# Where adaLN's rows, the norms and an expert's pieces are bound in the order of a transformer layer's kernel

## The chip, the cores and the metric

The kernel runs on one core of a Trainium2 chip. The metric is the device time of one execution in microseconds (us). A core has five engines with a queue of instructions each, worked off in order: TensorE (PE, with its weight loads as PEld), VectorE (DVE), ScalarE (ACT), GpSimd (POOL) and SyncE (SP), which here issues most of the DMA transfers. An instruction that waits holds up all that stands behind it on its own engine, and nothing else directly.

## What is computed

One layer over 2048 latent tokens of width 1024, float32, with 256 context tokens. The reference, cut to its path:

```python
mod = silu(c) @ w_ada + b_ada
sh1, sc1, g1, sh2, sc2, g2 = split(mod, 6)
h = layernorm(x) * (1 + sc1) + sh1
q, k, v, u, vg, ga, gb = split(h @ w_in)
y_attn = windowed_attention(q, k, v, context keys and values, sink, mask)
vc = layernorm(gelu(vg), gm_ln_g, gm_ln_b)        # chunks of 128 tokens, 8 groups of 64
y_gm = gelu(u) * (einsum('gpq,nqgc->npgc', gm_ws, vc) + gm_bs)
mix = (sigmoid(ga) * (y_attn @ w_pa) + sigmoid(gb) * (y_gm @ w_pb)) @ w_o
x = layernorm(ALPHA * x + g1 * mix, ln1_g, ln1_b)
h2 = layernorm(x) * (1 + sc2) + sh2
x = layernorm(ALPHA * x + g2 * mixture_of_experts(h2), ln2_g, ln2_b)   # top 2 of 32
```

## The kernel before

**Stages.** A first pass (0 to about 600 us) normalises the tokens, projects q, k and v and does the attention; it leaves `hT_d` (the modulated tokens, transposed), `oT_d` (attention output) and `vg_d` in DRAM. The second pass, `pass2`, takes the 2048 tokens as four groups g = 0..3 of 512 tokens, four tiles of 128 each, and starts its group 0 at about 600 us, group 1 at about 785. Then come the experts: `early_block` for the first of them, and from about 1490 us the experts' loop.

**Products.** A float32 product is made of three products of rounded halves: `split` (line 85) casts a piece to its high half on ScalarE (`Wh`, `hh`, `gh`) and subtracts that on VectorE for the low half (`Wl`, `hl`, `gl`); `mm3` (lines 741 to 743) multiplies high by high, low by high and high by low. A matmul of line 742 therefore needs a `Wl`, one of 741 a `Wh`. Weights pass through `piece` (line 729): one buffer `raw` of 128 x 1024, of which there are three (`RAW`), loaded by a DMA that SP issues. `Wh` and `Wl` have three buffers each, the PSUM banks `mm` four, `tr` two.

**A group.** `head(g)` forms the projection u from four `raw` pieces of `hT_d` and four of `wu`; `gelu_u` and four `norm_v` (a load `vg`, GELU, statistics, `vg` normalised by lines 784 and 785, split into `yl`) feed `spatial`, which for each of eight groups of channels does a product into `tr` and then line 840 on VectorE, the product with u into `yh`. Then a loop over f = 0..7, one eighth of the merged width each: `gate(g, f + 1, 0)`, for f = 0 also `mixers(g)` (transposes of `yh` by line 850 and their split into `gh` and `gl`) and `attended(g)`, then `between(g, f)`, `gate(g, f + 1, 1)`, `merge` and `behind`. `out_proj` evacuates `mm` into `rr` (line 906) at the end of groups 0 to 2; the last group has a planner of its own, `last_tiles`.

**The two kinds of side work.** In group 0 `between` issues one step of `rows_ada`, for f = 0..5. A step forms 512 entries of g1, sh2 or sc2: four pieces of `w_ada` through the same `raw` ring, eight VectorE instructions into `aacc` (lines 760 and 762), a split into `ah` and `al`; two matmuls and an addition (lines 774 to 777) follow as `finish` when `between` is called next. In groups 1 to 3 `between` issues for f = 0..3 the `norms` of one tile of the group before: load `x`, line 912 (`rr<-x,rr`), a layer norm of `rr` (statistics of line 94, the small ones of 98 and 99, the root of line 100 on GpSimd, lines 784 and 785), a store, a second norm into `x` and a second store. From f = 1 on the transposes and logits of the tile before it follow.

**What sets the order.** The program is written out as above, and a scheduler then orders each engine's instructions by a simulated timeline. `tc.issue_after(ins)` adds one rule to it: instructions that are traced inside the block and run on the engine of `ins` may not be issued ahead of `ins`. `st["mixed"]` is the last split of `attended`, on VectorE. The norms of each tile are bound by

```python
with tc.issue_after(st["mixed"]):
    h2s[t] = norms(t, rr[f])
```

and the scheduler places that split early, ahead of the spatial products, so all the norms may go there as well.

**The experts' loop.** The blocks of up to 128 tokens follow one another expert by expert. `prepare(s, p)` loads the weight piece p of expert s (`mraw`, 1 MB) and splits it into `mWh` and `mWl`; `rows` makes the stationary operand `xh` of the next block, `hidden` and `output` are its matmuls (`terms`, line 1612). `k.at[kp]` is the last matmul of the kp-th quarter of `hidden`. In block 1 the loop calls `prepare(1, 0)` and `prepare(1, 1)`, with no rule on their order.

Of the kernel before, what the change touches and what calls it, by code (L numbers as in the profile page):

```python
# [13 lines left out]
OP = mybir.AluOpType  # L14
# [690 lines left out]
def pass2(k):  # L705
    nc, tc, T = k.nc, k.tc, k.T
    k.late = k.ctx.enter_context(tc.tile_pool(name="late", bufs=1, reuse_waits="tile"))
    with ExitStack() as ctx:
# [16 lines left out]
        bst = c.tile([P, 8], F32, name="bst")  # L725
# [25 lines left out]
        def rows_ada(dst, cb, one):  # L751

            acc = wk.tile([P, 512], F32, name="aacc", tag="aacc", bufs=1)
            for kp in range(4):
                w = piece(T["ada2"][cb, :, 2 * kp:2 * kp + 2, :].rearrange("p a b -> p (a b)"))
                for j in range(2):
                    kc = 2 * kp + j
                    ws = w[:, j * 512:(j + 1) * 512]
                    if kc == 0:
                        nc.vector.tensor_scalar(acc, ws, k.sil[:, kc, 0:1], None, op0=OP.mult)  # L760
                    else:
                        nc.vector.scalar_tensor_tensor(acc, ws, k.sil[:, kc, 0:1], acc, op0=OP.mult, op1=OP.add)
            ah = wk.tile([P, 512], F32R, name="ah", tag="th", bufs=1)
            al = wk.tile([P, 512], F32R, name="al", tag="tl", bufs=1)
            split(k, ah, al, acc)
            if dst is None:
                d = wk.tile([P, 512], F32, name="sg", tag="sg", bufs=2 * AHEAD + 2)
                nc.sync.dma_start(d, bcast_row(T["b_ada"][2048 + cb * 512:2048 + (cb + 1) * 512], 512))
            else:
                d = dst[:, (cb % 2) * 512:(cb % 2 + 1) * 512]  # L770

            def finish():
                pr = tr_bank()
                nc.tensor.matmul(pr, ones, ah, start=True, stop=False)
                nc.tensor.matmul(pr, ones, al, start=False, stop=True)
                nc.vector.scalar_tensor_tensor(d, d, one, pr, op0=OP.add, op1=OP.add)
                if dst is None:
                    nc.sync.dma_start(k.g2_d[:, (cb % 2) * 512:(cb % 2 + 1) * 512], d[0:1, :])
            return finish
# [7 lines left out]
        st = {}  # L787
# [41 lines left out]
        def spatial(g):  # L829

            uy, vv = st[g][1], st["vv"]
            if g == 0:
                tc.keep_in_program_order(nc.sync.dma_start(bst, T["bst"]))
            ws = wsplit(T["wst"].rearrange("p g q -> p (g q)"))
            for gg in range(8):
                tp = tr_bank()
                sp = tp[:, 0:256].rearrange("p (i d) -> p i d", d=HD)
                cs = slice(gg * HD, (gg + 1) * HD)
                mm3(sp, [x[:, gg * P:(gg + 1) * P] for x in ws], (vv[:, 0, :, cs], vv[:, 1, :, cs]), True, True)
                nc.vector.scalar_tensor_tensor(uy[:, 1, :, cs], sp, bst[:, gg:gg + 1], uy[:, 0, :, cs],  # L840
                                               op0=OP.add, op1=OP.mult)

        def mixers(g):

# [313 lines left out]
        rr, h2s, turned, routes, wout, due = None, {}, {}, {}, {}, []  # L1158

        def between(g, f):  # L1160

            nonlocal g1, sh2, sc2, ln1g, ln1b, rws
            while due:
                due.pop(0)()
            if g == 0:
                if f < 6:
                    due.append(rows_ada(g1 if f < 2 else sh2 if f < 4 else sc2, f, 1.0 if f // 2 == 2 else 0.0))
                return
            t = 4 * (g - 1) + f
            if 1 <= f < 5:  # L1170
                turned[t - 1] = logit_rows(h2s[t - 1])
            if f < 4:
                with tc.issue_after(st["mixed"]):
                    h2s[t] = norms(t, rr[f])
            if g == 1 and f in (5, 6):
                due.append(rows_ada(None, f + 1, 0.0))
# [310 lines left out]
def moe(k):  # L1487
    nc, tc, T = k.nc, k.tc, k.T
    with ExitStack() as ctx:
# [40 lines left out]
        def prepare(s, p):  # L1530

            if s >= NE:
                return
            hi, lo = (weight(n, s, p) for n in "hl")
            split(k, hi, lo, raws[s, p])
            parts[s, p] = (hi, lo)
            if s or p < 4:
                load()
# [164 lines left out]
        for i in range(NBL):  # L1703
            s, _, _, last = blocks[i]
            hidden(i)
            gate(i)
            with tc.issue_after(k.at[3]) if not i else nullcontext():
                rows(i + 1)
                if not i:
                    early_output(1)  # L1710
            if i:
                gather(i + GA)
                output(i - 1)
                evacuate(i - 1)
            if last:
                ahead(s, 3)
            if i and blocks[i - 1][3]:
                prepare(s, 4)
                prepare(s, 5)
            if i == 1:  # L1720
                prepare(1, 0)
                prepare(1, 1)
            if i > 3:
                next(k.tables, None)
        k.gb = wr.tile([P, 2, D], F32, name="gb", tag="mraw", bufs=RAWS)
# [184 lines left out]
```

## Time and profile before

| | us |
|---|---|
| median of three runs | 2355.22 |
| lowest and highest | 2352.29, 2355.99 |
| the profiled execution's own time | 2353.14 |
| span of the profile (first to last instruction) | 2351.1 |

The mean granted TensorE clock of that execution was 0.977 of full speed. PE was busy for 2206.8 us, DVE for 1749.7, ACT for 1197.9, POOL for 622.1. "Idle before" of a group of instructions is the time its engine stood idle ahead of them, and a wait is put down to the work that released it. Idle time of an engine that nobody waits for costs nothing, so the tables of TensorE's waits come first, and the other engines' order of time is read where they point to.

### The profile page before, as it was taken

The page shows a single profiled execution, that of the slowest core. Times are in us where ns is not written, and L with a number is a line of the kernel's source. Part 1 is how long each engine was busy: PE and PEld are TensorE (multiplying, and loading weights), DVE is VectorE, ACT ScalarE, POOL GpSimd, SP SyncE. Part 2 cuts the span into 40 slices and gives each one's busy share as a digit, 9 for nine tenths or more (in the row PEclk, how much of TensorE's full clock was granted, in tenths as well). Part 3 has the DMA queues.
Part 4 walks back from the last instruction along what each step waited for, and adds up shares of the span by engine and source line. Part 5 has one row for each costly group of instructions (what it writes and reads, how often), then busy time and mean ns, then how long its engine had stood idle before and what let it go on. Part 6 is the DMA issues. An engine that isn't in the chain of part 4 may idle for free. (4 is left out here: it accounts for less than half of the span.)

```text
span 2351.1 us, 31795 instructions
## 1 busy us (share of the span) xinstructions
PE 2206.8 (94%) x11269; PEld 1813.8 (77%) x11269; DVE 1749.7 (74%) x3029; ACT 1197.9 (51%) x1673; POOL 622.1 (26%) x518
## 2 busy tenths in 40 slices
PE   7899999999999999999999999899999999999980
PEld 3789999997778788878887887587877777877760
DVE  4778888887675677577557858578898878696977
ACT  3566666655433333333424333356666666564755
POOL 1333333331000101011101113323353445243324
PEclk9899999999999999999999999899999999999995
DMA  8111111115674446544344434489998989797967
GB/s 313 64 59 59 55 59 42 41 42 170 197 239 153 152 144 185 161 151 150 112 156 153 153 117 188 152 271 322 338 339 290 330 280 331 234 360 235 337 215 295
DMA packets 126710, 449.34 MB, mean 191 GB/s; under 512 B 20763, under 2 KB 42195, under 8 KB 101973
## 3 DMA queue, kind: packets, MB, share of 16 engines
q1 hardware_dynamic: 113684, 405.29, 49.8%
q0 software_dynamic: 12864, 41.98, 7.5%
q8 instruction: 90, 1.47, 0.3%
q14 instruction: 72, 0.58, 0.1%
HBM read 382.66 MB, written 64.57 MB: 190 GB/s over the span
## 5 line engine op out<-in xcount | busy, mean ns | idle before, releaser
L85 DVE TENSOR_TENSOR mWl<-mraw,mWh 128x2048 fp32r<-128x2048 f32 x192 | 450.2, 2362 | 89.9 <-ACT mWh L85 89.0
L85 ACT CAST mWh<-mraw 128x2048 fp32r<-128x2048 f32 x192 | 363.7, 1909 | 176.0 <-PE h L1612 82.2
L100 POOL TENSOR_TENSOR mv<-mv,mhalf 128x1 f32<-128x1 f32 x58 | 56.7, 981 | 664.2 <-DVE mv L99 657.9
L1612 PE MATMUL h<-mWh,xh 128*128 128x512 f32 x784 | 218.2, 400 | 12.4 <-ACT xh L85 7.9
L85 DVE TENSOR_TENSOR Wl<-raw,Wh 128x1024 fp32r<-128x1024 f32 x140 | 170.4, 1220 | 77.5 <-ACT Wh L85 76.8
L85 ACT CAST Wh<-raw 128x1024 fp32r<-128x1024 f32 x140 | 146.1, 1047 | 139.0 <-PE mm L743 66.2
L1612 PE MATMUL h<-mWl,xh 128*128 128x512 f32 x784 | 214.7, 394 | 0.0
L742 PE MATMUL mm<-hh,Wl 128*128 128x512 f32 x512 | 201.1, 393 | 5.5 <-DVE Wl L85 5.5
L741 PE MATMUL mm<-hh,Wh 128*128 128x512 f32 x512 | 202.7, 396 | 2.3 <-ACT Wh L85 1.6
L743 PE MATMUL mm<-hl,Wh 128*128 128x512 f32 x512 | 200.8, 392 | 0.0
L1660 POOL DMA_INDIRECT acc_d<-yo,lst x48 | 144.1, 3003 | 153.6 <-DVE yo L1654 95.7
L1612 PEld LDWEIGHTS h<-mWh,xh 128*128 128x128 f32 x784 | 145.3, 189 | 46.5 <-ACT xh L85 9.8
L1612 PEld LDWEIGHTS h<-mWl,xh 128*128 128x128 f32 x784 | 146.8, 188 | 32.9
L383 PE MATMUL pj<-wq,hTh 128*128 128x256 f32 (+1 forms) x544 | 151.9, 355 | 1.6 <-DVE hTh L364 1.4
L1577 POOL DMA_INDIRECT xg<-h_d,lst x48 | 79.9, 1665 | 206.6 <-PE tr L1598 98.7
L85 ACT CAST ph<-pt 128x512 fp32r<-128x512 f32 x184 | 93.4, 520 | 73.4 <-PE pt L572 69.9
L1612 PE MATMUL h<-mWh,xl 128*128 128x512 f32 x464 | 127.0, 394 | 0.0
L548 ACT ACTIVATE Sb<-Sb,mx 128x641 f32<-128x641 f32 (+1 forms) x128 | 105.4, 824 | 40.3 <-DVE mx L543 31.3
L541 DVE CUSTOM_DVE_ANT_0 Sb<-S,mask,sink 128x640 f32<-128x640 f32 (+1 forms) x128 | 110.2, 861 | 18.9 <-PE S L537 15.8
L85 DVE TENSOR_TENSOR pl<-pt,ph 128x512 fp32r<-128x512 f32 x184 | 109.0, 604 | 19.2 <-ACT ph L85 17.4
L1612 PE MATMUL y<-mWh,gh 128*128 128x512 f32 x392 | 112.2, 406 | 8.1 <-ACT mWh L85 3.3
L742 PEld LDWEIGHTS mm<-hh,Wl 128*128 128x128 f32 x512 | 96.7, 189 | 26.4 <-DVE Wl L85 7.1
(385 smaller groups left out, 5371.9 us busy)
## 6 DMA issues: line engine op xcount, KB each, us to landing
mraw<-mw SPq DMA_DIRECT2D x192, 1024.0 KB, 7.3
raw<-wf SPq DMA_DIRECT2D x96, 512.0 KB, 3.7
raw<-ada SPq DMA_DIRECT2D x32, 512.0 KB, 4.8
raw<-wo SPq DMA_DIRECT2D x32, 512.0 KB, 4.2
x<-x SPq DMA_DIRECT2D x30, 512.0 KB, 4.3
x<-ada SPq DMA_DIRECT2D x16, 512.0 KB, 5.4
hT_d<-hf SPq DMA_DIRECT2D x32, 256.0 KB, 2.2
raw<-hT_d SPq DMA_DIRECT2D x16, 512.0 KB, 4.9
```

The costliest lines, as they stand in the source:

```text
L85: return k.nc.scalar.copy(hi, src), (eng or k.nc.vector).tensor_sub(lo, src, hi)
L100: nc.gpsimd.tensor_tensor(mv[:, 3:4], mv[:, 2:3], k.mhalf, op=OP.pow)
L383: ins = nc.tensor.matmul(box[0][:, :n], x[:, kc, ts], wpart(y, kc, slice(c0, c0 + n))[:, 0, :], start=q == 0, stop=q == 3 * KC - 1)
L541: nc.vector.tensor_tensor_reduce(x[:, :nk], S[:, :nk], mask[:, mi, :nk], 1.0, sink[:, h:h + 1], OP.add, OP.max, mx[:, s:s + 1])
L548: nc.scalar.activation(Sb[s][:, :nk + 1], Sb[s][:, :nk + 1], AF.Exp, bias=mx[:, 2 + s:3 + s], scale=1.0, accum_out=mx[:, 4 + s:5 + s])
L741: nc.tensor.matmul(out, lh, rh, start=first, stop=False)
L742: nc.tensor.matmul(out, ll, rh, start=False, stop=False)
L743: nc.tensor.matmul(out, lh, rl, start=False, stop=last)
L1577: ins = nc.gpsimd.indirect_dma_start(out=xg[i][0:n, :], out_offset=None, in_=k.h2_d[:, :], in_offset=bass.IndirectOffsetOnAxis(ap=place(i) ...
L1612: ins = nc.tensor.matmul(accs[m], a[:, ks], b[:, c0:c0 + 512], start=first and i + j == 0, stop=last and j == 1 and i == len(t) - 1)
L1660: nc.gpsimd.indirect_dma_start(out=k.acc_d[:, :], out_offset=bass.IndirectOffsetOnAxis(ap=l[:, 0:1], axis=0), in_=yo[0:n, :], in_offset=No ...
```

## The change

There are three parts. In group 0 the six steps of `rows_ada` are issued at f = 1..6 in place of f = 0..5, and bound behind `st["sp"]`, which is new: the last VectorE instruction of line 840, the end of the group's spatial mixing. In groups 1 to 3 the norms for f = 1, 2 and 3 are bound behind `st["sp"]` too; the first tile's (f = 0) stay behind `st["mixed"]`. In the experts' loop `prepare(1, 0)` and `prepare(1, 1)` are bound behind `k.at[3]`, which in block 1 is the last matmul of that block's `hidden`.

```diff
--- before.py
+++ after.py
@@ -837,8 +837,8 @@
                 sp = tp[:, 0:256].rearrange("p (i d) -> p i d", d=HD)
                 cs = slice(gg * HD, (gg + 1) * HD)
                 mm3(sp, [x[:, gg * P:(gg + 1) * P] for x in ws], (vv[:, 0, :, cs], vv[:, 1, :, cs]), True, True)
-                nc.vector.scalar_tensor_tensor(uy[:, 1, :, cs], sp, bst[:, gg:gg + 1], uy[:, 0, :, cs],
-                                               op0=OP.add, op1=OP.mult)
+                st["sp"] = nc.vector.scalar_tensor_tensor(uy[:, 1, :, cs], sp, bst[:, gg:gg + 1], uy[:, 0, :, cs],
+                                                          op0=OP.add, op1=OP.mult).ins
 
         def mixers(g):
 
@@ -1163,14 +1163,15 @@
             while due:
                 due.pop(0)()
             if g == 0:
-                if f < 6:
-                    due.append(rows_ada(g1 if f < 2 else sh2 if f < 4 else sc2, f, 1.0 if f // 2 == 2 else 0.0))
+                if 1 <= f < 7:
+                    with tc.issue_after(st["sp"]):
+                        due.append(rows_ada(g1 if f < 3 else sh2 if f < 5 else sc2, f - 1, 1.0 if f > 4 else 0.0))
                 return
             t = 4 * (g - 1) + f
             if 1 <= f < 5:
                 turned[t - 1] = logit_rows(h2s[t - 1])
             if f < 4:
-                with tc.issue_after(st["mixed"]):
+                with tc.issue_after(st["sp" if f else "mixed"]):
                     h2s[t] = norms(t, rr[f])
             if g == 1 and f in (5, 6):
                 due.append(rows_ada(None, f + 1, 0.0))
@@ -1718,8 +1719,9 @@
                 prepare(s, 4)
                 prepare(s, 5)
             if i == 1:
-                prepare(1, 0)
-                prepare(1, 1)
+                with tc.issue_after(k.at[3]):
+                    prepare(1, 0)
+                    prepare(1, 1)
             if i > 3:
                 next(k.tables, None)
         k.gb = wr.tile([P, 2, D], F32, name="gb", tag="mraw", bufs=RAWS)
```

VectorE, group 0, around the last two spatial products (the rows of line 840), before. The `aacc` rows are the second step of `rows_ada` (f = 1), `Wl` a weight piece's low half, `gl` the first splits of `mixers`:

```order
L762 SCALAR_TENSOR_TENSOR aacc_7528<-raw_7533,sil_96,aacc_7528 128x512 x2
L762 SCALAR_TENSOR_TENSOR aacc_7528<-raw_7537,sil_96,aacc_7528 128x512
L85 TENSOR_TENSOR Wl_7494<-raw_7491,Wh_7493 128x1024
L762 SCALAR_TENSOR_TENSOR aacc_7528<-raw_7537,sil_96,aacc_7528 128x512
L887 TENSOR_TENSOR sg_7211<-sg_7211,mm_7458 128x512
L840 SCALAR_TENSOR_TENSOR yh_6994<-tr_7309,bst_6993,yh_6994 128x4x64
L840 SCALAR_TENSOR_TENSOR yh_6994<-tr_7314,bst_6993,yh_6994 128x4x64
L762 SCALAR_TENSOR_TENSOR aacc_7528<-raw_7541,sil_96,aacc_7528 128x512 x2
L85 TENSOR_TENSOR gl_7358<-tr_7352,gh_7357 128x512
L85 TENSOR_TENSOR Wl_7552<-raw_7549,Wh_7551 128x1024
L85 TENSOR_TENSOR gl_7358<-tr_7361,gh_7357 128x512
```

The same place after the change:

```order
L85 TENSOR_TENSOR Wl_7434<-raw_7431,Wh_7433 128x1024
L840 SCALAR_TENSOR_TENSOR yh_6994<-tr_7299,bst_6993,yh_6994 128x4x64
L840 SCALAR_TENSOR_TENSOR yh_6994<-tr_7304,bst_6993,yh_6994 128x4x64
L85 TENSOR_TENSOR Wl_7473<-raw_7470,Wh_7472 128x1024
L887 TENSOR_TENSOR sg_7211<-sg_7211,mm_7437 128x512
L840 SCALAR_TENSOR_TENSOR yh_6994<-tr_7309,bst_6993,yh_6994 128x4x64
L840 SCALAR_TENSOR_TENSOR yh_6994<-tr_7314,bst_6993,yh_6994 128x4x64
L760 TENSOR_SCALAR aacc_7503<-raw_7504,sil_96 128x512
L762 SCALAR_TENSOR_TENSOR aacc_7503<-raw_7504,sil_96,aacc_7503 128x512
L85 TENSOR_TENSOR gl_7358<-tr_7352,gh_7357 128x512
L762 SCALAR_TENSOR_TENSOR aacc_7503<-raw_7508,sil_96,aacc_7503 128x512
L85 TENSOR_TENSOR gl_7358<-tr_7361,gh_7357 128x512
```

Ahead of the last products there is no `aacc` row any more; the first step of `rows_ada` starts right behind them, between them and among the `gl`.

VectorE, group 1, where the last `Wl` of its `head` stands (`Wl_8671`; the `vg` rows are the group's own norm of v, `rr_8288` is the first tile of the group before), before:

```order
L99 TENSOR_SCALAR mv_8803<-mv_8803 128x1
L784 SCALAR_TENSOR_TENSOR vg_8798<-vg_8798,mv_8803,sg_8702 128x512
L85 TENSOR_TENSOR Wl_8671<-raw_8668,Wh_8670 128x1024
L99 TENSOR_SCALAR mv_8816<-mv_8816 128x1
L784 SCALAR_TENSOR_TENSOR vg_8811<-vg_8811,mv_8816,sg_8702 128x512
L94 BN_STATS st_8952<-rr_8288 128x6 x2
L785 SCALAR_TENSOR_TENSOR vg_8798<-vg_8798,mv_8803,sg_8704 128x512
L85 TENSOR_TENSOR Wl_8735<-raw_8732,Wh_8734 128x1024
```

The same place after:

```order
L99 TENSOR_SCALAR mv_8803<-mv_8803 128x1
L784 SCALAR_TENSOR_TENSOR vg_8798<-vg_8798,mv_8803,sg_8702 128x512
L94 BN_STATS st_8952<-rr_8288 128x6
L99 TENSOR_SCALAR mv_8816<-mv_8816 128x1
L784 SCALAR_TENSOR_TENSOR vg_8811<-vg_8811,mv_8816,sg_8702 128x512
L85 TENSOR_TENSOR Wl_8671<-raw_8668,Wh_8670 128x1024
L94 BN_STATS st_8952<-rr_8288 128x6
L785 SCALAR_TENSOR_TENSOR vg_8798<-vg_8798,mv_8803,sg_8704 128x512
```

One of the two statistics rows of `rr_8288`, a small addition and line 784 of the second `vg` now stand ahead of this `Wl`, and the norm of the first tile is no longer behind it as a whole.

VectorE, group 1, from the `Wl` ahead of the first spatial products (`Wl_8873`; `rr_8289` and `x_9093` are the second tile of the group before), before:

```order
L99 TENSOR_SCALAR mv_9099<-mv_9099 128x1
L784 SCALAR_TENSOR_TENSOR rr_8289<-rr_8289,mv_9099,ln1g_8240 128x1024
L785 SCALAR_TENSOR_TENSOR x_8949<-x_8949,mv_8965,sh2_7489 128x1024
L785 SCALAR_TENSOR_TENSOR rr_8289<-rr_8289,mv_9099,ln1b_8242 128x1024
L85 TENSOR_TENSOR Wl_8873<-raw_8870,Wh_8872 128x1024
L94 BN_STATS st_9106<-rr_8289 128x6 x2
L840 SCALAR_TENSOR_TENSOR yh_8548<-tr_8830,bst_6993,yh_8548 128x4x64
L840 SCALAR_TENSOR_TENSOR yh_8548<-tr_8835,bst_6993,yh_8548 128x4x64
L98 BN_AGGR mv_9109<-st_9106 128x2
```

The same place after, up to the first products, and then what follows the last two products:

```order
L784 SCALAR_TENSOR_TENSOR x_8949<-rr_8288,mv_8965,sc2_7722 128x1024
L85 TENSOR_TENSOR Wl_8827<-raw_8824,Wh_8826 128x1024
L785 SCALAR_TENSOR_TENSOR x_8949<-x_8949,mv_8965,sh2_7468 128x1024
L85 TENSOR_TENSOR Wl_8873<-raw_8870,Wh_8872 128x1024
L840 SCALAR_TENSOR_TENSOR yh_8548<-tr_8830,bst_6993,yh_8548 128x4x64
L840 SCALAR_TENSOR_TENSOR yh_8548<-tr_8835,bst_6993,yh_8548 128x4x64
```

```order
L840 SCALAR_TENSOR_TENSOR yh_8548<-tr_8865,bst_6993,yh_8548 128x4x64
L912 SCALAR_TENSOR_TENSOR rr_8289<-x_9093,rr_8289 128x1024
L85 TENSOR_TENSOR Wl_9119<-raw_9116,Wh_9118 128x1024
L85 TENSOR_TENSOR gl_8909<-tr_8903,gh_8908 128x512
L94 BN_STATS st_9096<-rr_8289 128x6 x2
L85 TENSOR_TENSOR gl_8909<-tr_8912,gh_8908 128x512
L98 BN_AGGR mv_9099<-st_9096 128x2
L99 TENSOR_SCALAR mv_9099<-mv_9099 128x1
L784 SCALAR_TENSOR_TENSOR rr_8289<-rr_8289,mv_9099,ln1g_8236 128x1024
L785 SCALAR_TENSOR_TENSOR rr_8289<-rr_8289,mv_9099,ln1b_8238 128x1024
L94 BN_STATS st_9106<-rr_8289 128x6 x2
L85 TENSOR_TENSOR Wl_9152<-raw_9149,Wh_9151 128x1024
```

The second tile's norm has left the place ahead of `Wl_8873` and stands behind the last products, among `Wl` and `gl` rows; the third and fourth tiles' norms stood behind them before as well. Groups 2 and 3 have the same pattern. The block of the third part issues ScalarE, VectorE and SP instructions, while `k.at[3]` is one of TensorE; at its place the order of no engine differs between the two kernels.

## Rows read from the trace of the kernel before

**Rows 1.** The page's first part: busy us, share of span, instructions:

```profile
PE 2206.8 (94%) x11269; PEld 1813.8 (77%) x11269; DVE 1749.7 (74%) x3029; ACT 1197.9 (51%) x1673; POOL 622.1 (26%) x518
```

**Rows 2.** Stretches: us, busy PE, PEld, DVE, ACT, POOL, clock, DMA, GB/s:

```profile
600.00:640.00 40.00, 35.03 (x157) 28.66 (x156) 24.76 (x38) 12.68 (x16) 0.55 (x1) 0.91 0.62 195
640.00:780.00 140.00, 139.26 (x610) 114.06 (x609) 89.33 (x114) 44.09 (x55) 0.00 (x0) 1.00 0.59 188
780.00:840.00 60.00, 55.31 (x252) 44.51 (x251) 45.52 (x67) 24.01 (x31) 7.47 (x6) 1.00 0.46 149
```

**Rows 3.** TensorE's waits in 600 to 640: us in total, times, longest:

```profile
PE tr L850 <- DVE yh L840: 2.6, 1, 2.6
PE mm L741 <- ACT Wh L85: 1.6, 1, 1.6
PE mm L742 <- DVE Wl L85: 0.8, 1, 0.8
```

**Rows 4.** Two short stretches behind waits, columns as in rows 2:

```profile
611.00:614.50 3.50, 3.46 (x8) 2.72 (x9) 2.58 (x4) 1.04 (x1) 0.00 (x0) 0.52 0.94 353
624.90:628.40 3.50, 3.49 (x12) 2.96 (x13) 2.89 (x5) 2.11 (x3) 0.00 (x0) 0.53 0.86 297
```

**Rows 5.** TensorE's waits in 780 to 1280, groups 1 to 3:

```profile
PE mm L742 <- DVE Wl L85: 4.5, 3, 1.5
PE mm L743 <- DVE mv L99: 2.3, 3, 0.9
...
PE tr L850 <- DVE yh L840: 1.4, 3, 0.5
```

**Rows 6.** VectorE in group 0: start, us, instruction, idle before it:

```profile
621.32 0.75 DVE L762 SCALAR_TENSOR_TENSOR aacc<-raw,sil,aacc 128x512 f32<-128x512 f32 x1 [1.34 <-DMA raw<-ada]
...
624.38 0.87 DVE L840 SCALAR_TENSOR_TENSOR yh<-tr,bst,yh 128x256 f32<-128x256 f32 x2
```

**Rows 7.** VectorE in group 1, ahead of the spatial products:

```profile
819.32 1.28 DVE L785 SCALAR_TENSOR_TENSOR rr<-rr,mv,ln1b 128x1024 f32<-128x1024 f32 x1
820.52 1.22 DVE L85 TENSOR_TENSOR Wl<-raw,Wh 128x1024 fp32r<-128x1024 f32 x1
```

**Rows 8.** The page's DMA issues: count, size, us to landing:

```profile
raw<-wf SPq DMA_DIRECT2D x96, 512.0 KB, 3.7
```

**Rows 9.** ScalarE in the experts' first blocks:

```profile
1501.20 1.90 ACT L85 CAST mWh<-mraw 128x2048 fp32r<-128x2048 f32 x1 [9.62 <-DMA mraw<-mw]
```

**Rows 10.** TensorE behind group 1's last spatial products:

```profile
838.11 1.09 PE L850 MATMUL tr<-ident,yh 128*128 128x128 f32 x8 [0.47 <-DVE yh L840]
...
840.01 0.39 PE L741 MATMUL mm<-hh,Wh 128*128 128x512 f32 x1
...
844.57 0.39 PE L743 MATMUL mm<-hl,Wh 128*128 128x512 f32 x1
```

**Rows 11.** VectorE in group 1's head:

```profile
789.16 1.22 DVE L912 SCALAR_TENSOR_TENSOR rr<-x,rr 128x1024 f32<-128x1024 f32 x1
...
801.36 1.22 DVE L85 TENSOR_TENSOR Wl<-raw,Wh 128x1024 fp32r<-128x1024 f32 x1
802.50 0.15 DVE L99 TENSOR_SCALAR mv<-mv 128x1 f32<-128x1 f32 x1
802.56 0.74 DVE L784 SCALAR_TENSOR_TENSOR vg<-vg,mv,sg 128x512 f32<-128x512 f32 x1
803.22 1.28 DVE L94 BATCH_NORM_STATS2 st<-rr 128x6 f32<-128x512 f32 x2
```

**Rows 12.** GpSimd's roots in group 1:

```profile
802.79 0.92 POOL L100 TENSOR_TENSOR mv<-mv,mhalf 128x1 f32<-128x1 f32 x1 [0.94 <-DVE mv L99]
807.83 1.46 POOL L100 TENSOR_TENSOR mv<-mv,mhalf 128x1 f32<-128x1 f32 x1 [4.12 <-DVE mv L99]
```

**Rows 13.** VectorE behind group 1's last spatial products:

```profile
839.91 1.28 DVE L85 TENSOR_TENSOR gl<-tr,gh 128x512 fp32r<-128x512 f32 x2
```

**Rows 14.** TensorE's waits in 1485 to 1525:

```profile
PE h L1612 <- ACT xh L85: 6.0, 1, 6.0
```

## The prediction, made before the changed kernel ran

> **What bounds the kernel now.** I read the engines' shares first: TensorE's matmuls are busy 94% of the span, VectorE (DVE) 74% [rows 1]. So a change of order pays only where TensorE waits, and I looked for its waits in the two places that the change touches, the start of group 0 and the starts of groups 1 to 3. The table by stage shows the contrast: in 640 to 780 us matmuls are busy 139.26 of 140 us, in 600 to 640 only 35.03 of 40 [rows 2]. The table of waits gives the 5.0 us of group 0 in three entries, 2.6 for the transposes behind the last spatial product (the `yh` of line 840), 1.6 and 0.8 for one weight piece's `Wh` and `Wl` [rows 3]. Behind each of these two places the clock is down to about half: 0.52 granted in 611.0 to 614.5 and 0.53 in 624.9 to 628.4, though nothing waits in them [rows 4]. In groups 1 to 3 together the same view gives 4.5 us for a `Wl`, three times alike, 2.3 for a norm's `mv`, also three times, and 1.4 for `yh` [rows 5].
>
> Who holds these up is in VectorE's order of time. In group 0 a step of the adaLN sum (`aacc`, line 762) comes up after 1.34 us of waiting for its DMA, at 621.32. A `Wl`, another `aacc` and a product stand behind it, and only at 624.38 the two `yh` for which TensorE waits its 2.6 us [rows 6]. In group 1 the `Wl` that TensorE waits 1.5 us for starts at 820.52, directly behind a norm instruction of 1.28 us (`rr`) that belongs to the group's second tile [rows 7].
>
> **The change part by part.** *adaLN of group 0.* The six steps go from f = 0..5 to f = 1..6, and their VectorE instructions stand behind the last `yh`. Nothing is saved in work: each step keeps its four weight DMAs, eight `aacc`, two splits and two matmuls. What goes is the place. The first step's four DMAs stood ahead of two weight pieces in the ring of three `raw` buffers, and that gave the 1.6 and 0.8 us; its `aacc` stood ahead of `yh`, and that gave the 2.6. So 5.0 us of waits go, except about 0.5 us, which is what the same place costs in groups 1 to 3 without any adaLN ahead of it (1.4 us in three [rows 5]). With the waits I expect the half clock to go: (1 - 0.52) x 3.5 = 1.7 and (1 - 0.53) x 3.5 = 1.6, 3.3 us at most. Gain 5.0 + 3.3 - 0.5 = 7.8 us.
>
> What it costs: the second gate of f = 2 now finds four adaLN pieces ahead of it in the ring. From the last `yh` on, VectorE does four `aacc` of at most 0.75 [rows 6] and two `gl` before that gate's buffer is free, some 4.2 us; its DMA takes 3.7 [rows 8], the cast to `Wh` half of the 1.90 that twice the size takes [rows 9], `Wl` 1.22 [rows 7]: ready at about 10.1 us. TensorE has eight transposes and two products (1.9 us, from 838.11 to 840.01), 24 matmuls at 0.228 us (20 steps from 840.01 to 844.57) and another eight transposes with their products (1.8 us) before it wants `Wh`, at about 9.2, and some 0.7 later `Wl` [rows 10]. A wait of nothing to 1.5 us, if the DMA is a slow one; I take 0.5. The sixth step now falls on f = 6: five such steps lie in 640 to 780 us, where 0.7 us in all is not busy [rows 2], so 0.2 us. Group 0: -7.8 + 0.7 = -7.1 us.
>
> *Norms of groups 1 to 3.* The first tile's norm stays; the second tile's (`rr` of line 912 on) goes behind the last `yh`. Ahead of the `Wl` of 820.52 there then stands half a norm less (two statistics, two small ones, two of about 1.28), some 4 us, so it is early, and 4.5 us go [rows 5, 7]. A second place gets worse, and I see it only in the order: the head's last `Wl`, at 801.36, for which TensorE waits 0.9 us (the table puts it down to the `mv` just before it [rows 5]), now stands behind one statistics instruction (half of 1.28), an addition of 0.15 and one 0.74 us instruction that stood behind it before, +1.5 us [rows 11]. Against that, line 912 of the second tile is no longer ahead of the buffers that the `vg` loads wait for: it took 1.22 us there at 789.16, and the whole chain starts that much earlier [rows 11]. Net +0.3 us in each group, between 0 and +1.5. Groups 1 to 3: -4.5 + 0.9 = -3.6 us.
>
> Behind the last `yh` the second tile's norm now lies among the `gl` that TensorE needs. VectorE's row there is line 912 1.22, `Wl` 1.22, `gl` 0.64, statistics 1.28, `gl` 0.64, about 0.35 of small ones, GpSimd's root up to 1.46, two of 1.28, statistics 1.28, `Wl` 1.22, `gl` 0.64: 12.5 us until the third `gl` [rows 7, 11 to 13]. By TensorE's order 59 products of 0.228 and 16 transposes come first, 13.5 and some 2 us [rows 10]. The cover is 3 us, so I price it at nothing. Its queue on SP: the second tile's two stores move behind five further weight loads and are issued when no load behind them is due yet.
>
> *Second expert's pieces.* The block that is bound to `k.at[3]` issues ScalarE, VectorE and SP instructions only, and the edge is made for instructions on the engine of `k.at[3]`, TensorE, alone. The order on every engine shows the two pieces where they were, so 0 us. ScalarE's cast there waits 9.62 us for its weights [rows 9] and the next block's `xh` stands behind it, which costs TensorE 6.0 us; I expect these to stay [rows 14].
>
> **Sum.** -7.1 - 3.6 = -10.7 us. The profiled execution took 2353.1 us (span 2351.1 and 2.0 around it), so 2342.4. The three runs have a median of 2355.2, 2.1 above it: forecast 2344.5 us. The experts' loop behind the change keeps its order but for one weight piece near the end, and its first loads are requested when the last group's output products are done, so I take the gain to pass through.
>
> **The rivals.** *Given back (no change).* The waits only move: `vg` is not earlier, so each head piece costs the full 1.5 (+4.5 against -4.5), and the gate of f = 2 waits its 1.5 us and brings the half clock back (3.3). Left are -5.0 + 0.5 + 1.5 + 0.2 = -2.8 us: 2352.4. For it: the head piece is in the order. Against it: in 780 to 840 us waits of 0.9 and 1.5 us left the clock at 1.00 [rows 2, 5].
>
> *The clock stays down (a smaller gain).* A new wait at f = 2 keeps group 0 at half clock as long as before, so the 3.3 us stay lost: -5.0 + 0.5 + 0.7 - 3.6 = -7.4, 2347.8. For it: the half clock came twice in 40 us behind waits of 2.4 and 2.6 us [rows 3, 4]. Against it: the new wait is the smaller. One rule puts the gain near this. The Trainium skill, "Perfetto Trace Analysis", section "Identifying the Most-Contended Engine", calls matmul busy time a poor measure of TensorE's headroom and the busy share of weight loads a good one. Loads are busy 28.66 of 40 us in group 0's start and 114.06 of 140 behind it [rows 2]; by that there are only (0.815 - 0.717) x 40 = 3.9 us to gain there, an estimate that makes the sum -3.9 + 0.7 - 3.6 = -6.8 us, 2348.4. The trace speaks against taking it whole, since a load at half clock counts as busy for longer.
>
> *Slower.* The cover of 3 us behind the last `yh` does not hold. VectorE works in order; if one of the two `Wl` there gets its `Wh` over 3 us late, all of the second tile's norm stands before a `gl` on the path: 1.22 + 1.28 + 0.35 + 1.46 + 3 x 1.28 = 8.15 us in each of three groups. -10.7 + 24.4 = +13.7: 2369. Against it: the loads for both are requested before the group's last `yh`. For it: GpSimd's root takes 0.92 us beside an instruction of 0.74 and 1.46 among longer ones [rows 12], and the moved chain has two.
>
> *The third part takes hold.* Were the two pieces behind the first block, ScalarE would reach `xh` without that cast, for at most the 6.0 us that TensorE waits there [rows 14]: 2338.5. Against it stands the order.
>
> **How the numbers follow.** Forecast 0.57, clock 0.13, given back 0.18, slower 0.07, third part 0.05. What a measurement can tell from no change is about 0.2%, 4.7 us: faster is under 2350.5, slower over 2359.9. The forecast's own range is 2342 to 2349 (the wait at f = 2 between 0 and 1.5, the head piece between 0 and +1.5 in each group), and it is faster, as are the clock's case and the third part's: 0.75. The given-back case is within 0.2%. For the spread of the runs I move 0.03 from the first: faster 0.72, same 0.20, slower 0.08. The range of eight in ten takes in nearly all of the third part and most of the given-back case: 2339 to 2353.
>
> **What would show it.** In 600 to 640 us no wait for line 840 over 0.8 us and none for `Wh` or `Wl` before it, with a granted clock of 1.0; no wait of 1.5 us for `Wl` some 18 us ahead of each group's last `yh`; the wait for the head's last `Wl` 0.9 to 2.4 us in each group, 0.9 before; ScalarE's 9.6 us wait in the experts' first blocks unchanged. I am wrong if new waits for `gl` stand behind the spatial products, if the clock is half in group 0 all the same, or if the experts' loop takes back what the groups gave.

## The result, and the profile after

The changed kernel runs in 2339.32 us (median of four runs, 2338.42 to 2345.82) against 2355.6 before (of four runs): a ratio of 0.9939, 95% interval 0.9918 to 0.9960, so 14 us faster (9 to 19). Two more comparisons (e4 and e11 below) gave 0.9938 (0.9923 to 0.9952) and 0.9942 (0.9928 to 0.9955). One execution of e4, of 10075.89 us, counts as a slow run and is in no ratio. The forecast of 2344.5 us had the sign and most of the gain; the time lies 5 us under it, at the low end of the range of eight in ten (2339 to 2353). The profiled execution took 2345.8 us (span 2344.0).

TensorE's waits of the changed kernel from 586 to 640 us, around group 0's spatial products (columns: waits of whom for whom, us in total, times, longest; they answer to [rows 3]):

```profile
PE mm L742 <- DVE mv L99: 0.8, 1, 0.8
PE tr L850 <- DVE yh L840: 0.5, 1, 0.5
PE mm L741 <- ACT gh L85: 0.2, 1, 0.2
PE mm L741 <- ACT Wh L85: 0.2, 1, 0.2
```

The 2.6 us for `yh` have become 0.5, the 1.6 us for `Wh` are gone. The 0.8 for a `Wl` is still there (the table names the `mv` that stands behind it on VectorE; the `Wl` is the row at 604.67, 1.23 us, between the first and the second pair of `yh` rows as before). The prediction expected none there. The stretches of [rows 2] in the changed kernel, same columns:

```profile
600.00:640.00 40.00, 38.33 (x179) 30.55 (x179) 26.01 (x41) 14.46 (x19) 0.55 (x1) 1.00 0.49 150
640.00:780.00 140.00, 137.15 (x601) 112.48 (x600) 93.43 (x118) 45.34 (x56) 0.00 (x0) 1.00 0.62 200
780.00:840.00 60.00, 57.76 (x271) 47.43 (x270) 42.41 (x65) 22.77 (x31) 8.59 (x6) 1.00 0.43 133
```

Matmuls are busy for 38.33 us between 600 and 640 in place of 35.03, at a granted clock of 1.00 in place of 0.91. VectorE around the last spatial product, which answers to [rows 6]:

```profile
613.81 1.23 DVE L85 TENSOR_TENSOR Wl<-raw,Wh 128x1024 fp32r<-128x1024 f32 x1 [2.21 <-ACT Wh L85]
614.96 0.69 DVE L887 TENSOR_TENSOR sg<-sg,mm 128x512 f32<-128x512 f32 x1
615.56 0.87 DVE L840 SCALAR_TENSOR_TENSOR yh<-tr,bst,yh 128x256 f32<-128x256 f32 x2
616.35 0.48 DVE L760 TENSOR_SCALAR aacc<-raw,sil 128x512 f32<-128x512 f32 x1
```

The product stands at 615.56, with 2.21 us in which VectorE stood idle two rows ahead of it; the adaLN step begins behind it. TensorE's waits in 770 to 1280 us (the groups lie some 10 us earlier), which answer to [rows 5]:

```profile
PE mm L743 <- DVE Wl L85: 3.6, 3, 1.5
PE mm L741 <- DVE rr L906: 3.4, 3, 2.0
PE tr L850 <- DVE yh L840: 1.4, 3, 0.5
PE mm L742 <- DVE Wl L85: 1.0, 1, 1.0
PE mm L741 <- ACT Wh L85: 0.8, 1, 0.8
PE mm L741 <- ACT gh L85: 0.7, 3, 0.2
```

The three waits of 1.5 us for `Wl` ahead of the spatial products are gone. The 3.6 us under line 743 are the head's last `Wl`, 2.3 before (in the head the weights are the second operand of `mm3`, so there it is line 743 that needs a `Wl`, and not 742 as in the gates). No wait for `gl` has come. In the experts' first blocks the cast of `mraw` still waits, now 13.21 us, and TensorE 8.7 us for `xh` ([rows 9, 14]):

```profile
1492.97 1.90 ACT L85 CAST mWh<-mraw 128x2048 fp32r<-128x2048 f32 x1 [13.21 <-DMA mraw<-mw]
```

```profile
PE h L1613 <- ACT xh L85: 8.7, 1, 8.7
```

### The profile page after: what moved, and what is told of

It reads as the page before. It is cut to its first block, busy times and chain, and to the rows that moved or that the text cites. A ratio compares the mean times of both kernels' runs of the same rounds, so it can differ in the third digit from the quotient of the medians.

```text
span 2344.0 us, 31796 instructions
## 1 busy us (share of the span) xinstructions
PE 2206.1 (94%) x11269; PEld 1810.5 (77%) x11269; DVE 1747.5 (75%) x3029; ACT 1197.1 (51%) x1671; POOL 635.8 (27%) x518
## 5 line engine op out<-in xcount | busy, mean ns | idle before, releaser
L100 POOL TENSOR_TENSOR mv<-mv,mhalf 128x1 f32<-128x1 f32 x58 | 68.0, 1174 | 642.5 <-DVE mv L99 608.8
L1613 PE MATMUL h<-mWh,xh 128*128 128x512 f32 x784 | 219.4, 401 | 13.8 <-ACT xh L85 10.8
L1578 POOL DMA_INDIRECT xg<-h_d,lst x48 | 85.4, 1780 | 209.8 <-PE tr L1599 102.9
```

Source lines behind the costliest of these rows:

```text
L100: nc.gpsimd.tensor_tensor(mv[:, 3:4], mv[:, 2:3], k.mhalf, op=OP.pow)
L1578: ins = nc.gpsimd.indirect_dma_start(out=xg[i][0:n, :], out_offset=None, in_=k.h2_d[:, :], in_offset=bass.IndirectOffsetOnAxis(ap=place(i) ...
L1613: ins = nc.tensor.matmul(accs[m], a[:, ks], b[:, c0:c0 + 512], start=first and i + j == 0, stop=last and j == 1 and i == len(t) - 1)
```

## The experiments

All stretches are read from TensorE's timeline by marks that every kernel has: the first product of group 0's first gate (line 741, at 590.2 us before), the first transposes of `yh` (line 850) of groups 1, 2 and 3, the experts' first product (`h`), and the 101st of those. The table and the expectations call the first mark the start of head 0; group 0's head itself lies ahead of it, from 563.8 to 590.2 us before, and not from about 600 as I had put it above. In us, one profiled execution each:

| kernel | start of head 0 | to group 1 | to 2 | to 3 | to experts | head 0 to experts | experts' first 100 | rest |
|---|---|---|---|---|---|---|---|---|
| before | 590.2 | 247.9 | 218.8 | 217.9 | 208.9 | 893.6 | 46.4 | 821.0 |
| e3, before's order | 587.2 | 246.3 | 218.8 | 217.9 | 209.4 | 892.4 | 46.8 | 818.4 |
| e12, before's order | 590.0 | 245.5 | 219.7 | 218.0 | 209.4 | 892.6 | 47.4 | 817.4 |
| e1, adaLN only | 588.4 | 241.0 | 219.0 | 217.2 | 209.5 | 886.6 | 48.5 | 818.2 |
| e2, norms only | 590.1 | 245.6 | 220.6 | 215.2 | 209.1 | 890.5 | 49.6 | 825.1 |
| the change | 586.8 | 240.9 | 218.7 | 216.2 | 210.2 | 886.0 | 48.0 | 823.2 |
| e4, the change | 591.1 | 239.4 | 217.6 | 215.8 | 210.1 | 882.8 | 47.6 | 815.2 |
| e11, the change | 589.3 | 238.4 | 218.5 | 215.6 | 209.5 | 882.1 | 47.7 | 821.7 |
| e5, pieces on ScalarE | 589.5 | 245.6 | 219.8 | 220.5 | 209.4 | 895.3 | 37.5 | 823.6 |
| e6, change and e5 | 585.9 | 239.9 | 218.8 | 215.7 | 209.1 | 883.4 | 40.2 | 823.4 |
| e7, all norms behind | 590.7 | 243.2 | 225.1 | 219.0 | 211.6 | 899.0 | 47.7 | 820.8 |
| e8, bound, not shifted | 591.7 | 248.1 | 219.1 | 218.4 | 210.8 | 896.4 | 46.9 | 819.0 |
| e9, shifted, not bound | 590.4 | 248.9 | 221.4 | 218.7 | 213.0 | 902.0 | 44.6 | 816.9 |
| e10, e6 and first norm later | 589.9 | 237.7 | 218.0 | 216.8 | 209.6 | 882.1 | 37.4 | 821.9 |

The columns outside the groups spread by some 5 us (first) and 10 us (last) between kernels that are the same there; the stretch between head 0 and the experts is steady within 4 us where the order is the same up to the experts.

### The parts by themselves: e1, e2, e3, e4

e1 is the change without its second and third part, e2 without the first and third, e3 with the third alone, e4 the whole.

> Only the first part: the six adaLN steps at f = 1..6 and behind the last spatial product. My theory (the wait for `yh`, the two weight waits and the half clock of group 0 go): 7.1 us faster than before, between 6 and 8; in the trace no wait over 0.8 us for line 840 and a granted clock of 1.0 in the start of group 0. Rival, the clock stays down or the ring makes a new wait at f = 2: 3 to 4 us faster. Rival, the loop of experts takes up what arrives earlier: group 0 is shorter in the trace, the whole is within 2 us of before.

Measured: 0.9959 (0.9945 to 0.9973), 9.7 us faster (6 to 13). In 600 to 640 us the granted clock is 1.00, the wait for `yh` 0.5 us, that for the `Wl` 0.3. Head 0 to group 1 takes 241.0 us, 4.5 to 6.9 less than in the three profiles of before's order (before, e3, e12).

> Only the second part: the norms at f = 1, 2, 3 behind the last spatial product in groups 1 to 3. My theory: the three waits of 1.5 us for `Wl` go, the head's last `Wl` costs 0.3 us more in each group: 3.6 us faster. Rival, the head's `Wl` costs the full 1.5 us more in each: 0. Rival, the norm behind the last product stands in the way of `gl`: some us slower, with a wait for `gl` in groups 1 to 3.

Measured: 0.9981 (0.9970 to 0.9992), 4.5 us faster (2 to 7); head 0 to the experts takes 890.5 us, 2.4 less than the mean of those three (892.9). The waits for the `Wl` ahead of the spatial products are gone; the head's last `Wl` costs 3.8 us in three groups. No wait for `gl`. Neither rival holds.

> Only the third part as it is written, bound to a matmul. My theory: the order of every engine is that of before, so the time is that of before within 0.1% (2 us), and what differs is what two programs with the same order differ by. Rival, the edge takes hold in some way that the order does not show: up to 6.0 us faster, with ScalarE's 9.6 us wait for `mraw` behind the casts to `xh`.

Measured: 1.0008 (0.9993 to 1.0022). ScalarE's cast waits 12.14 us for `mraw`, TensorE 7.8 us for `xh`, as before.

> The whole change once more, beside its parts on the same chip. My theory: the parts add, so this is the sum of the three, 10.7 us faster than before by my working; the first result, some 16 us, was then 5 us of something that the parts do not have. Rival, the parts are not additive, since the loop of experts starts at another phase of its weight transfers: the whole differs from the sum by over 3 us, and the trace shows the difference behind 1470 us.

Measured: 0.9938 (0.9923 to 0.9952), 14.6 us. The parts add: 9.7 + 4.5 - 1.9 = 12.3 us, within the intervals.

### Which half of the first part does it: e8 and e9

```diff
-                if 1 <= f < 7:
+                if f < 6:
                     with tc.issue_after(st["sp"]):
-                        due.append(rows_ada(g1 if f < 3 else sh2 if f < 5 else sc2, f - 1, 1.0 if f > 4 else 0.0))
+                        due.append(rows_ada(g1 if f < 2 else sh2 if f < 4 else sc2, f, 1.0 if f // 2 == 2 else 0.0))
```

That is e8 against e1: bound, at the old f. e9 is e1 without the `with` line: at the new f, not bound.

> The adaLN steps stay at f = 0..5 and are only bound behind the last spatial product. My theory: the binding takes away the 2.6 us wait for `yh` and the half clock behind it (1.6 us), while the first step's four pieces still stand ahead of two weight pieces in the ring of `raw`, now until behind the last product, so a wait for `Wh` and `Wl` of 2.4 us or more stays with its half clock: at most 4 us faster, and no gain if that wait grows by what the pieces are held longer (some 10 us from the last product on against some 9 us of TensorE's work). Rival (the shift does nothing, the binding is all): as fast as both together, some 10 us.

Measured: 0.9993 (0.9981 to 1.0005), no change. TensorE's waits from head 0 to 640 us in e8:

```profile
PE mm L741 <- ACT Wh L85: 5.4, 2, 5.2
PE tr L850 <- DVE gl L85: 1.7, 2, 1.1
PE tr L741 <- DVE yh L840: 0.2, 1, 0.2
PE tr L850 <- DVE yh L840: 0.2, 1, 0.2
```

The wait for `yh` is gone, and one of 5.2 us for a `Wh` has come. ScalarE's cast waits for its transfer, and SyncE's queue, which issues the loads of `raw`, waits up to 11.6 us for an `aacc` to free a buffer (600 to 624 us, first line):

```profile
SPq L729 <- DVE aacc L762: 16.6, 4, 11.6
```

```profile
620.02 1.04 ACT L85 CAST Wh<-raw 128x1024 fp32r<-128x1024 f32 x1 [3.49 <-DMA raw<-wf]
```

The two stretches behind (columns as in [rows 2]) are at half clock, 0.51 and 0.50:

```profile
615.50:621.00 5.50, 0.41 (x4) 0.10 (x1) 4.32 (x7) 1.56 (x3) 0.00 (x0) 0.51 0.72 230
621.00:625.00 4.00, 3.88 (x8) 2.71 (x9) 2.57 (x3) 1.64 (x3) 0.00 (x0) 0.50 0.93 330
```

That is the second case of my theory, no gain since the wait grew by what the pieces are held longer. The rival, that the binding is all, is out.

> The adaLN steps at f = 1..6 without the binding, nothing else changed: the other half of part one. The binding alone measured nothing, since its four pieces kept the ring. Theory A (the ring place costs, so the shift alone carries the weight waits): the waits of 1.6 and 0.8 us for `Wh` and `Wl` ahead of the last product are gone with their half clock, some `aacc` still stands ahead of a `yh`, so part of the 2.6 us stays: 4 to 6 us from the start of group 0's head products to its first transpose of `yh` of the 6 us that both together give. Theory B (only both together do anything): the stretch from the start of the head to the first transpose is as long as before, 34 to 35.6 us, against 28.6 to 29.3 with both.

Measured: 1.0012 (0.9997 to 1.0027), no gain. The stretch to the first transposes of `yh` takes 35.6 us. The waits for `Wh` are gone here, and those for `yh` are 6.5 us in place of 2.6:

```profile
PE tr L850 <- DVE yh L840: 4.7, 1, 4.7
PE tr L741 <- DVE yh L840: 1.8, 2, 1.6
```

VectorE in e9 ahead of the last product, two `aacc` rows of 1.54 that wait for their own transfers:

```profile
618.25 1.54 DVE L762 SCALAR_TENSOR_TENSOR aacc<-raw,sil,aacc 128x512 f32<-128x512 f32 x2 [2.55 <-DMA raw<-ada]
619.71 0.87 DVE L840 SCALAR_TENSOR_TENSOR yh<-tr,bst,yh 128x256 f32<-128x256 f32 x2
621.58 1.54 DVE L762 SCALAR_TENSOR_TENSOR aacc<-raw,sil,aacc 128x512 f32<-128x512 f32 x2 [1.00 <-DMA raw<-ada]
...
625.43 0.87 DVE L840 SCALAR_TENSOR_TENSOR yh<-tr,bst,yh 128x256 f32<-128x256 f32 x2
```

So theory B: neither half gives anything that can be told from no change, both together give all. Bound without the shift, the step holds the ring; shifted without the binding, the scheduler still lets its sums in ahead of the products.

### The third part where it takes hold: e5 and e6

```diff
-                    split(k, th[:, sl], tl[:, sl], tp)
+                    k.last = split(k, th[:, sl], tl[:, sl], tp)
...
                 rows(i + 1)
                 if not i:
+                    k.x1 = k.last
...
-                with tc.issue_after(k.at[3]):
+                with tc.issue_after(k.x1[0].ins), tc.issue_after(k.x1[1].ins):
                     prepare(1, 0)
```

e5 has this on the kernel before, e6 on the changed one.

> Before with the third part alone, but bound to engines that the pieces use: `prepare(1, 0)` and `prepare(1, 1)` behind the ScalarE cast and the VectorE subtraction of block 1's `xh`. In the order this moves one ScalarE row, the cast of `mraw` that waited for its transfer, behind hs and the two casts to `xh`; VectorE's order is unchanged. TensorE waited 6.0, 7.8 and 9.3 us for `xh` there in the three profiles that have before's place for it. Theory A (that cast is the cause): the wait for `xh` is under 1 us and the kernel is 6 to 9 us faster than before. Theory B (the experts' loop is fed by its weight transfers, so what is won at its start is waited for later): the wait goes, other waits for `mWh` or `mWl` take its place, and the whole gain is under 3 us.

Measured: 0.9946 (0.9934 to 0.9959), 12.7 us faster (10 to 16). ScalarE in e5:

```profile
1480.92 10.93 ACT L85 CAST mWh<-mraw 128x2048 fp32r<-128x2048 f32 x6
1496.10 1.28 ACT L1630 ACT_TABLE_LOAD   x1 [4.25 <-issue]
1497.39 0.60 ACT L1630 ACTIVATE hs<-h 128x512 f32<-128x512 f32 x1
1497.89 1.07 ACT L85 CAST xh<-tr 128x512 fp32r<-128x512 f32 x2
1503.88 1.91 ACT L85 CAST mWh<-mraw 128x2048 fp32r<-128x2048 f32 x1 [4.93 <-DMA mraw<-mw]
```

The casts to `xh` come ahead of the one that waits for `mraw`. TensorE's wait for `xh` is gone, and in its place stand no others in that stretch than one of 2.2 us for `gh`, which before had too (2.3), and one of 0.6 for `gl`, as in e3 and e12. The experts' first 100 products take 37.5 us in place of 46.4 to 47.4. Theory A, with more gained than its 6 to 9 us.

> The whole change with its third part bound as in the run on ScalarE. Theory A: the gains add, 14.6 us from the first two parts as measured and 6 to 9 us more, so 21 to 24 us faster than before, about 2332 us. Theory B: no faster than the whole change as it is, 14 to 16 us.

Measured: 0.9900 (0.9884 to 0.9917), 2334.09 us, 23.6 us faster than before (20 to 27), some 9 us faster than the change as it is: theory A.

### How much fits behind the last product: e7 and e10

e7 is e2 with `st["sp"]` for f = 0 too.

> The second part alone, with the norm of the first tile (f = 0) bound behind the last spatial product too. It puts 1.22 + 1.28 + 1.28 = 3.8 us more of VectorE's work ahead of the third `gl` and takes 1.28 and 0.15 away, 15.0 us in place of 12.5, against 15.5 us of TensorE's products. My theory (the cover holds): no new wait for `gl`, and since nothing of a norm stands ahead of the head's last `Wl`, its wait is back at 0.9 us in each group: 1 us faster than the norms' part alone, some 5 us faster than before. Rival (slower: the cover does not hold): waits for `gl`, or for the `Wl` and the transposes of the first logits, of some us in each of three groups, and the run is slower than the norms' part alone by 5 us or more.

Measured: 1.0007 (0.9998 to 1.0017), so some 6 us slower than e2 (0.9981): the rival. The waits of e7 in 770 to 1280 us:

```profile
PE mm L741 <- DVE rr L906: 5.6, 6, 1.5
PE mm L741 <- ACT Wh L85: 3.7, 1, 3.7
PE lg L937 <- ACT th L85: 1.5, 2, 0.7
```

The head's last `Wl` is waited for nowhere. For `gl` neither; the norms' backlog comes out later: the first logits wait for `th`, and one `Wh` is 3.7 us late in the place where group 1's two steps of adaLN (f = 5, 6) use the ring. VectorE there waits 2.45 us for a `vg` with an `aacc` behind it, and ScalarE's cast for its transfer:

```profile
937.17 0.69 DVE L94 BATCH_NORM_STATS2 st<-vg 128x6 f32<-128x512 f32 x1 [2.45 <-ACT vg L825]
937.78 0.74 DVE L762 SCALAR_TENSOR_TENSOR aacc<-raw,sil,aacc 128x512 f32<-128x512 f32 x1
```

```profile
942.14 1.04 ACT L85 CAST Wh<-raw 128x1024 fp32r<-128x1024 f32 x1 [1.03 <-DMA raw<-wf]
```

SyncE's queue stood 7.5 us there ahead of the loads of `vg`, until a product of the logits (925 to 946 us, first line):

```profile
SPq L824 <- PE lg L937: 7.5, 1, 7.5
```

Whether the held ring makes the 3.7 us, or that wait in the queue that issues the loads of `raw` too, was not tested. My price looked only at the third `gl`.

e10 is e6 with the first norm ahead of the spatial products, but behind the last split of v:

```diff
-            split(k, vv[:, 0, i, :], vv[:, 1, i, :], vg)
+            st["nv"] = split(k, vv[:, 0, i, :], vv[:, 1, i, :], vg)[1].ins
...
-                with tc.issue_after(st["sp" if f else "mixed"]):
+                with tc.issue_after(st["sp" if f else "nv"]):
```

> The whole change with its third part bound on ScalarE, and the first tile's norm (f = 0) bound behind the last split of v in place of `mixed`, so that none of it stands ahead of the head's last `Wl` (waits of 0.8 to 1.5 us in each group with the change, 0.7 to 0.9 before). Theory A: these waits fall to 0.7 us or less, the norm still fits ahead of the first spatial product, and the kernel is 1 to 3 us faster than the version without this edit, about 25 us faster than before. Theory B: the norm, started later, now meets the `Wl` ahead of the spatial products, as the second tile's did before, and a wait of up to 1.5 us in each of three groups takes back what was won: within 2 us of the version without this edit.

Measured: 0.9893 (0.9878 to 0.9908), 2332.37 us, the fastest here: 25.2 us (22 to 29) under before. Its longest waits in 770 to 1280 us:

```profile
PE mm L741 <- DVE rr L906: 5.2, 6, 1.1
PE mm L742 <- DVE Wl L85: 1.6, 2, 1.0
```

The wait for the head's last `Wl` (3.1 us in e6) is gone, while line 906 at the head's start is waited for six times in place of three, and 0.6 of the 1.6 us stand ahead of group 3's spatial products (at 1246), the wait of which theory B spoke. From head 0 to the experts that leaves 1.3 us (883.4 to 882.1). Against e6 the timing does not tell the two apart, and so it does not tell theory A from B.

### Where the rest of the gain is: e11 and e12

> The whole change again. From the head of group 0 to the experts' first product its profiles are 9.7 us shorter than those with before's order (means of 3 and 4 profiles), close to the 10.7 of the prediction, while timed runs gave 14.6 us. Theory A (run to run differences in the first pass and the late experts' loop, which the change leaves alone): the stretch is again 8 to 11 us shorter, and the timed gain lies between 8 and 14. Theory B (something outside that stretch gets faster with the change): the timed gain is again 14 us or more, with the stretch at 8 to 11.

Measured: 0.9942 (0.9928 to 0.9955), 13.7 us (11 to 17), with the stretch at 882.1, 10.8 us under the mean of before's order. By their letter that is theory A, 0.3 us from B.

> Before's order once more (the third part as written, which moves no instruction). Three profiles with that order have 892.4, 893.5 and 895.3 us from group 0's head to the experts' first product, against 882.9, 882.1 and 886.1 with the whole change, 10.0 us on the mean, and the timed gain is 14 us. Theory A (the three profiles fell on short ones of a stretch that varies): this profile's stretch is 897 us or more. Theory B (the stretch is 10 us, and the rest of the timed gain lies outside it): the stretch is again 892 to 896, and what varies from run to run is the first pass and the end of the experts' loop. In both, the time is that of before within 0.1%.

Measured: 1.0000 (0.9989 to 1.0010), with the stretch at 892.6: theory B. Between head 0 and the experts the change gives 892.9 - 883.6 = 9.3 us (three profiles each), by the timing 14. The profiles show no gain outside: the start is the same (589.1 on the mean of either), the experts' first 100 products take 0.9 us longer with the change, the rest spreads from 815 to 823. But the three profiled executions of before's order were faster than the medians of their runs (by 2.1, 8.4 and 2.8 us), those of the change 6.5 slower, 1.4 faster and equal. So the 14 of the timing are met by no profile of a middling execution of before, and where such an execution spends the 4 to 5 us stays open. A hint is TensorE's mean granted clock. In the timed executions it is 0.9760 with before and 0.9778 with the change (26 and 5 executions, e4's comparison), and 0.9755 and 0.9772 (15 and 5, e11's); in the three profiled executions of either order it is 0.9767. By my estimate, 0.0017 of some 2350 us, 4 us of clock may be what the profiles miss.

## Why the prediction was right, and where not

**Group 0 (-7.1 us).** Right in size: e1 gave 4.5 to 6.9 us in the stretch to group 1, 9.7 us (6 to 13) timed. The granted clock went to 1.00 with the waits, as forecast. Not all of the 4.5 us of waits went: the 0.8 for a `Wl` ahead of the last products stayed in two of the change's three profiles (none in e11). The place that I priced for a new wait, the second gate of f = 2, has its `Wl` done at 626.83 (the row at 625.60, 1.23 us), 10.4 us behind the last `yh` (616.43); I had said about 10.1. TensorE waits 0.2 us for that piece's `Wh` (at 625.62) and not for its `Wl`; I took 0.5. A wait of 0.8 us for a `Wl` that the sum did not have came one step later, at 646 (TensorE's waits in 617 to 770 us of the changed kernel, first line):

```profile
PE mm L742 <- DVE Wl L85: 0.8, 1, 0.8
```

What the prediction had wrong is the split of the 5.0 us: 2.4 to the ring and 2.6 to VectorE's order, as if each had its own cause and could be taken away alone. In e8 the wait for `yh` goes and one of 5.2 us for a `Wh` comes, in e9 the waits for `Wh` go and those for `yh` grow to 6.5: either half of the edit only moves the wait from one side to the other. I also gave the 2.6 us to the first step's `aacc`; the rows ahead of the last `yh` are the second step's.

**Norms (-3.6).** Right: 4.5 us (2 to 7) timed, 2.4 in the stretch. The wait for the `Wl` ahead of the spatial products went whole, the head's last `Wl` rose by (3.6 - 2.3) / 3 = 0.4 us in each group (with 3.1 and 1.8 us in e4 and e11, by 0.3 and by nothing), where I had said 0.3. Two entries of 1.0 and 0.8 us for `Wl` and `Wh` at 932 to 935 were not in the sum, and e2 has them too (1.0 and 0.8), so they come with the norms. They lie at the two adaLN steps of group 1, in the same ring, which the sum did not look at; that these make them was not tested.

**Behind the last product (0).** Right for one norm: no wait for `gl`. e7 shows the edge that the rival spoke of, at one norm more, but with waits for `Wh` and `th` and not for `gl`. So the forecast that one norm fits was right, and the place where a second one costs was not foreseen.

**The third part (0).** Right: e3 and e12 measure 1.0008 and 1.0000. The rival in which it takes hold was priced at 6.0 us "at most", the wait alone; made to take hold it gives 9 us in the trace. The price left out the half clock that comes with the wait, which the same prediction had counted in group 0. The experts' first 100 products before, and in them a stretch behind the wait for `xh` (columns as in [rows 2]):

```profile
1483.80:1530.20 46.40, 38.11 (x155) 29.10 (x154) 23.30 (x19) 16.46 (x15) 10.03 (x6) 0.89 0.62 199
1505.50:1508.90 3.40, 3.37 (x8) 2.70 (x9) 3.40 (x6) 0.47 (x1) 0.38 (x1) 0.51 0.10 32
```

and the first 100 in e5:

```profile
1484.80:1522.30 37.50, 34.78 (x155) 26.92 (x154) 22.66 (x19) 15.75 (x14) 8.77 (x6) 1.00 0.73 246
```

Of the 8.9 us between the two the wait makes 6.0. At the full clock the same matmuls are busy for 3.3 us less (34.78 for 38.11), and the wait for `gl` takes 0.6 back. In e3 and e12 the wait was longer than in the one profile that I had, 7.8 and 8.3 us.

**The sum.** -10.7 us against 9.3 in the stretch that it speaks of. The forecast's own range, 2342 to 2349 (by the two terms that it names, 2343 to 2349), missed the time by 3 us on the fast side, since the timing gives 4 to 5 us more than the profiles; no term of the sum can be named for it. That the time lies within the wider range is in that part luck.

**The other rivals.** The clock did not stay down (1.00 in 600 to 640 us of the change, e1, e4 and e11). To group 0's first `yh` transposes 34.7 us became 29.3, 5.4 less. The smaller gain that the Trainium skill's rule gave ("Perfetto Trace Analysis", "Identifying the Most-Contended Engine"), an estimate of 3.9 us for group 0's start by the busy share of weight loads, is too small here. In the trace of before a weight load took 0.33 us in 611.5 to 614.4, at half clock, and 0.19 from 614.8 on, so its busy share hid part of what there was to gain. Given back was wrong: the head's last `Wl` rose by 0.4 us and not 1.5, the gate of f = 2 waited 0.2, and the experts' loop took little back. Of the 9.3 us by which the experts' first product comes earlier, 8.4 are left behind the first 100 of them.

## What to carry to other kernels

Where side work disturbs a tight stretch through a shared ring and through an engine's order, both have to be moved past it; move one, and the wait only changes its name, so test the halves before you credit either. An order edge holds only on the engine of the instruction that it is bound to: look up which engines the bound block uses, and read the order to see that a row has moved. Price a wait with the half clock that comes with it: the row of the wait said 6 us, and taking it away gave 9.

## What was not expected of the hardware

The granted clock fell to 0.56 (610.5 to 614.0 us in e12) behind two waits of 0.8 us each:

```profile
610.50:614.00 3.50, 3.50 (x11) 2.73 (x10) 2.03 (x4) 0.68 (x1) 0.00 (x0) 0.56 0.95 335
```

In the changed kernel it stayed at 1.00 at the start of group 1, behind a wait of 2.0 us (line 906, until 775.81) and one of 1.5:

```profile
775.00:800.00 25.00, 22.66 (x98) 18.21 (x99) 17.28 (x29) 11.30 (x16) 3.90 (x3) 1.00 0.46 139
```

In e11, the same kernel once more, TensorE waited 1.8 us in that place (until 776.03), and there the clock fell:

```profile
777.00:780.40 3.40, 3.40 (x10) 2.59 (x9) 1.33 (x2) 1.79 (x2) 0.00 (x0) 0.52 0.51 192
```

So with one order of instructions the clock, 2.4 GHz when granted in full, once fell to its lower level of 1.2 behind a wait and once did not, and it fell behind the shorter of the two: the length of a wait alone does not tell. What sets it off was not tried.
